# A width-31 depthwise convolution as matmuls over 4 time phases x 32 channels, mixed with the projections around it

## The chip, the cores, the metric

One Trainium2 chip, all 8 cores, one sequence of the batch on each core; nothing is exchanged between cores. The metric is the device time in microseconds (us) of the slowest core. Some runs here show a slow state, in which the cores of one die (or both) have a lower granted TensorE clock and take longer (the kernel before once took 7153.55 us, with clocks of 0.81 on die 0 and 0.90 on die 1, against 0.97 in its runs of 6121 to 6132 us).

## The reference, cut to what matters

Four layers on x of shape (8, 4096, 1024). Each has a token mixer and a feed-forward. The mixer of layer 1 is the Conformer block, which the change rewrites; layers 0 and 3 have a width-3 gated convolution, layer 2 pooling.

```python
def conformer_conv(h, w_pw1, b_pw1, conv_w, conv_b, ln_g, ln_b, w_pw2, b_pw2):
    p = h @ w_pw1 + b_pw1                            # (B, S, 2D)   first projection
    a, gt = jnp.split(p, 2, axis=-1)
    u = a * jax.nn.sigmoid(gt)
    v = causal_dwconv(u, conv_w) + conv_b            # each channel alone, 31 taps
    v = jax.nn.silu(layernorm(v, ln_g, ln_b))        # norm over the 1024 channels
    return v @ w_pw2 + b_pw2                         # second projection
# per layer: x += g1 * mixer(modulated rmsnorm(x));  x += g2 * swiglu(modulated rmsnorm(x))
```

## The kernel before

Channels lie on partitions, time on the free axis. A stage goes over the sequence in four passes of 1024 tokens; a pass is a list of *units* (one weight block each), each emitted in two halves of 512 tokens (`nt`). bf16 matmuls, fp32 residual. The kernel is traced by line, and all projections share one helper (line 601 before, 627 after), so groups are told apart by their tiles.

The Conformer block before, cut:

```python
def units_B(st):
    # first projection, 256 columns of weights per unit (line 705: sigmoid, line 707: product)
    ... e.activation(sg_t[:, k, :], gt, AF.Sigmoid, bias=..., scale=1.0)
    ... e.scalar_tensor_tensor(U[:, 30:542], a, bias, sg_t[:, k, :], ALU.add, ALU.mult)

    def mk_conv(j):                      # channel chunk j: 31 diagonal weights of 128x128 (line 720)
        def conv(pe):
            for kk in range(31):
                ins = pe.matmul(bk, slab[:, kk * 128:(kk + 1) * 128], U[:, kk:kk + 512],
                                start=(kk == 0), stop=(kk == 30))
    def emit_ln(nt, u):                  # fp32 mean, line 738: 8 matmuls of 512 columns with ones
        ...                              # then Square, two Vector passes, Silu (line 761)
    for m in range(4):
        mk_in(m); mk_conv(2 * m); mk_conv(2 * m + 1)
    unit(st, emit_ln)
    for m in range(2):
        mk_out(m)                        # second projection + residual (lines 621, 623)
```

Work for the following pass (its loads of x, its RMS sums, its norm) and the conversions of later weights are *tasks* that are spread over the units and run after the second half of a unit:

```python
a, b = sts[k]["first"], sts[k]["end"]            # in units
spread(steps[:2], t0, t0 + 1)                    # the loads
spread(steps[2:12], t1, t2)                      # Square + sum (lines 511, 514)
spread(steps[12:], t2, b - LAG - ...)            # the norm
...
u["emit"](1, u["cell"])
for fn in todo.pop(j, []):                       # tasks once per unit
    fn()
```

The sum of the RMS norm is one matmul with a matrix of ones behind each Square: TensorE waits there when the Square comes late (121 us in layer 0, in the waits below).

Of the kernel before, what the change touches and what calls it, by code (L numbers as in the profile page):

```python
# [12 lines left out]
D = 1024  # L13
# [3 lines left out]
F = 2816  # L17
# [5 lines left out]
NEH = 96  # L23

def _vec_layout():
    off = {}
    n = 0

    def add(name, w=8):
        nonlocal n  # L30
        off[name] = n
        n += w

    for i in range(4):
        add(f"nmg{i}")
        add(f"nfg{i}")
        add(f"adab{i}", 48)
    for j in range(2):
        add(f"acw{j}", 24)
    add("bb1", 16)  # L40
    add("bcw", 248)
    add("bcb")
    add("blg")
    add("blb")
    add("bb2")
    add("psc")
    add("fg")
    add("invcnt", 64)
    return off, n
# [3 lines left out]
def _sub_slabs(i, part):  # L53
# [5 lines left out]
    if kind == 1:  # L59
        return [("bpw1", 4096), ("bconv", 3968), ("bconv", 3968)] * 4 + [("bpw2", 4096)] * 2  # L60
    return [("cgrp", 2048)]

def _slab_table():
# [3 lines left out]
    for i in range(4):  # L67
        for part in "MF":
# [64 lines left out]

def _pack_vecs(inp):
# [13 lines left out]
    put("bcw", np.concatenate([_colvec(inp["b_conv_w"][0][k]) for k in range(31)], axis=1))  # L148
    put("bcb", _colvec(inp["b_conv_b"][0]))
    put("blg", _colvec(inp["b_ln_g"][0]))  # L150
    put("blb", _colvec(inp["b_ln_b"][0]))
# [31 lines left out]
class Prog:  # L183
# [7 lines left out]
    def op(self, eng, fn, reads=(), writes=(), sem=None, inc=1, after=()):  # L191
# [33 lines left out]
        for b in writes:  # L225
# [4 lines left out]
STAGES = ([("M", 0, s) for s in range(NPAIR)] + [("F", 0, s) for s in range(NPAIR)]  # L230
          + [("M", 1, s) for s in range(NPAIR)] + [("F", 1, s) for s in range(NPAIR)]
          + [("CF", 2, s) for s in range(NPAIR)]
          + [("M", 3, s) for s in range(NPAIR)] + [("F", 3, s) for s in range(NPAIR)])

# [3 lines left out]
def build():  # L238
# [6 lines left out]
    ident_d = nc.dram_tensor("ident", [128, 128], F32, kind="ExternalInput").ap()  # L245
# [6 lines left out]
    with es:  # L252
# [7 lines left out]
        scr_t = sb("scr", [128, 5, 532], F32)  # L260
        tmp_t = sb("tmp", [128, 4, 512], F32)
        sg_t = sb("sg", [128, 2, 512], F32)
        ada_t = sb("ada", [128, 3, 512], F32)
        junk = sb("junk", [128, 512], BF16)
# [8 lines left out]
        haloB = sb("haloB", [128, 8, 30], BF16)  # L273
        haloC = sb("haloC", [128, 8, 15], F32)
        ones_bf = sb("ones_bf", [128, 128], BF16)
        ones_f = sb("ones_f", [128, 128], F32)
        ident_bf = sb("ident_bf", [128, 128], BF16)
        small = sb("small", [128, 20], F32)
        psum = es.enter_context(nc.psum_tensor("psum", [128, 8, 512], F32))
# [7 lines left out]
        semnames = ["pe", "act", "dve", "pool", "vec", "idn", "cin"]  # L287
# [23 lines left out]
        identb = Buf("ident")  # L311
        cbcb = Buf("cbc")
        junkb = Buf("junk")
        rawb = Buf("raw")
        modb = [[Buf(f"mod{i}_{q}") for q in range(6)] for i in range(4)]
        derb = [[Buf(f"der{i}_{q}") for q in range(3)] for i in range(4)]
        haloAb = [[Buf(f"hA{l}_{c}") for c in range(8)] for l in range(2)]
        haloBb = [Buf(f"hB{c}") for c in range(8)]
# [3 lines left out]
        ctr = dict(bank=0, tmp=0, sg=0, scr=0, ub=0)  # L322
# [6 lines left out]
        def bank():  # L329
            k = nxt("bank", 6)  # L330
            return psum[:, k, :], bankb[k]
# [8 lines left out]
        scr_flat = scr_t[:, :, :].rearrange("p a b -> p (a b)")  # L340

# [4 lines left out]
        def v32(t):  # L346
            return hid2[:, t * 1024:(t + 1) * 1024].bitcast(F32), [hidb[t][0], hidb[t][1]]

        def utile():
            k = nxt("ub", 6)  # L350
            return scr_flat[:, k * 272:(k + 1) * 272].bitcast(BF16), [scrb[q] for q in range(k * 272 // 532, (k * 272 + 271) // 532 + 1)]
# [10 lines left out]
        P.op("dve", lambda e: e.memset(ones_f[:, :], 1.0 / D), writes=[constb])  # L362
# [29 lines left out]
        for (part, i, s) in STAGES:  # L392
            for p in part.replace("C", "M"):
                for q in range(len(SLABS[(i, p)])):
                    seq.append((i, p, s, q))
        wstate = dict(loaded=0, used=0, done=0)

        def load_slab(g):
# [7 lines left out]
            elif s == 0 and name == "bconv":  # L406
                def mkdiag(e):
                    for kk in range(31):
                        ins = e.tensor_scalar(wring[:, k, kk * 128:(kk + 1) * 128], ident_bf[:, :], vcol("bcw", kk * 8 + bconv_chunk(q), 1), None, ALU.mult)
                    return ins  # L410

                P.op("dve", mkdiag, reads=[vecsb, identb], writes=[wb[k]])
# [6 lines left out]
        def bconv_chunk(q):  # L419
            n = 0  # L420
            for r in range(q):
                if SLABS[(1, "M")][r][0] == "bconv":
                    n += 1
            return n

# [5 lines left out]
        def next_slab(expect):  # L431
            g = wstate["used"]
            assert seq[g][0:2] == expect, (g, seq[g], expect)
# [10 lines left out]
        def ada_mul(i, t, src, bufs):  # L444
            eh = SECTIONS[t // 16] * 16 + t % 16
            hf = eh % 2
            P.op("dve", lambda e: e.scalar_tensor_tensor(junk[:, :], src, 1.0, cbc[:, hf * 512:(hf + 1) * 512], ALU.mult, ALU.mult,  # L447
                                                         accum_out=raw[:, eh:eh + 1]),
                 reads=bufs + [cbcb], writes=[junkb, rawb])
# [181 lines left out]
        def unit(st, fn, nslabs=0):  # L631
            units.append(dict(emit=fn, nslabs=nslabs, st=st, cell={}))

        def get_slab(u, nt, expect):
            if nt == 0:
                u["slab"] = next_slab(expect)
            return u["slab"]

        def units_A(st):
# [5 lines left out]
            def mk_in(j):  # L645
                def emit(nt, u):
                    slab, slabb = get_slab(u, nt, (i, "M"))
# [21 lines left out]
                unit(st, emit, 1)  # L669

            def mk_out(m):
                def emit(nt, u):
                    slab, slabb = get_slab(u, nt, (i, "M"))
# [4 lines left out]
                unit(st, emit, 1)  # L678
# [6 lines left out]
        def units_B(st):  # L685
            i, s, hk = st["i"], st["s"], st["hk"]
            g1 = modT[:, i, 16:24]
            h_rhs = lambda k, nt: hbuf[:, hk, k, tsl(nt)]
            ut = {}

            def mk_in(m):
                def emit(nt, u):
                    slab, slabb = get_slab(u, nt, (i, "M"))
                    for q in range(2):
                        j = 2 * m + q
                        U, Ub = utile()
                        ut[(j, nt)] = (U, Ub)
                        if s == 0 and nt == 0:
                            P.op("dve", lambda e: e.memset(U[:, 0:30], 0.0), writes=Ub)
                        else:  # L700
                            P.op("dve", lambda e: e.tensor_copy(U[:, 0:30], haloB[:, j, :]), reads=[haloBb[j]], writes=Ub)
                        a, ab = proj_group(slab, slabb, q * 256, 8, 512, h_rhs, hb[hk], nt)
                        gt, gtb = proj_group(slab, slabb, q * 256 + 128, 8, 512, h_rhs, hb[hk], nt)
                        k = nxt("sg", 2)
                        P.op("act", lambda e: e.activation(sg_t[:, k, :], gt, AF.Sigmoid, bias=vcol("bb1", 8 + j, 1), scale=1.0),  # L705
                             reads=[gtb, vecsb], writes=[sgb[k]])
                        P.op("dve", lambda e: e.scalar_tensor_tensor(U[:, 30:542], a, vcol("bb1", j, 1), sg_t[:, k, :], ALU.add, ALU.mult),  # L707
                             reads=[ab, sgb[k], vecsb], writes=Ub)
                        P.op("dve", lambda e: e.tensor_copy(haloB[:, j, :], U[:, 512:542]), reads=Ub, writes=[haloBb[j]])
                unit(st, emit, 1)  # L710

            def mk_conv(j):
                def emit(nt, u):
                    slab, slabb = get_slab(u, nt, (i, "M"))
# [299 lines left out]
```

## Time and profile before

| | kernel before |
|---|---|
| median of 3 runs (range) | 6277.73 us (6123.72 to 7171.87) |
| fastest run | 6123.72 us |
| layer 0: mixer, feed-forward | 648, 928 us |
| layer 1: Conformer block, feed-forward | 1019, 992 us |
| layer 2: pooling and feed-forward | 1576 us |
| layer 3 to the end | 957 us |

The stretches are means over the eight cores of the profiled run. Each feed-forward or pooling layer is counted from its first gate x up product, so a stretch holds the handover to the next one. Layer 1's Conformer block is a sixth of the time; the views that show why are in the prediction below. Two Vector operations, by groups (line, engine, operation, tiles, shapes, count; then busy us and mean ns of one; then the idle time before them and what ended it):

```profile
L707 DVE SCALAR_TENSOR_TENSOR scr<-psum,vecs_sb,sg 128x512 bf16<-128x512 f32 x64 | 48.1, 751 | 511.0 <-ACT sg L705 510.5
L623 DVE TENSOR_TENSOR xres<-xres,tmp 128x512 f32<-128x512 f32 x64 | 43.9, 692 | 64.3 <-ACT tmp L621 63.9 <-issue 0.3
```

And TensorE's largest wait in layer 0 (waits of core 5, 0 to 666 us; the sum in us, how many, and the longest):

```profile
PE psum L514 <- ACT sqr L511: 121.2, 32, 48.5
```

The Square of x comes late for the RMS sum 32 times, by 121 us in all, 48 of them in one wait at the start.

### The profile page before, as it was taken

The numbers are of one execution on the slowest core, as the hardware profiler recorded it, in microseconds if no ns is written. First come the engines' busy times: TensorE is split into PE (matmuls) and PEld (weight loads), VectorE is DVE, ScalarE is ACT, GpSimd is POOL, SyncE is SP. The second block draws the span as 40 slices with busy tenths as digits, with TensorE's granted clock in tenths as the row PEclk, the third lists the DMA queues.
The fourth block names the chain that finished last, engine by engine and source line by source line (L and its number), as shares of the span: only waits on it lengthen the run. The fifth ranks groups of instructions, "written<-read, shape, count | busy, mean of one in ns | idle before, by whom it ended". The sixth has DMA issues, their size and how long they took to land.

```text
span 6137.7 us, 75215 instructions; the slowest of 8 cores (6107.0 to 6137.7 us)
## 1 busy us (share of the span) xinstructions
PE 5627.6 (92%) x25408; PEld 2504.6 (41%) x25408; DVE 2323.0 (38%) x4470; ACT 1668.4 (27%) x2530; POOL 457.7 (7%) x854
## 2 busy tenths in 40 slices
PE   3788999999989888899999979788799999999998
PEld 1333444444434333344444434333344444444443
DVE  4565432332331312223323345453624665233232
ACT  2222222222142433422222232313231222223221
POOL 1111010110000000001101001010100010000000
PEclk9899999999999999999999989899999999999999
DMA  7887444543424333156555234343545453233232
GB/s 179 198 205 189 155 147 144 181 139 107 143 77 141 104 107 120 63 156 205 154 166 177 87 117 135 128 129 126 147 126 157 141 162 136 97 134 103 96 110 73
DMA packets 201833, 837.86 MB, mean 137 GB/s; under 512 B 24032, under 2 KB 24032, under 8 KB 170592
## 3 DMA queue, kind: packets, MB, share of 16 engines
q1 hardware_dynamic: 135744, 544.60, 27.1%
q0 software_dynamic: 65712, 288.45, 18.3%
q8 instruction: 211, 3.46, 0.2%
q14 instruction: 166, 1.36, 0.1%
HBM read 791.83 MB, written 218.37 MB: 165 GB/s over the span
## 4 chain that ended last, share of the span: by engine, by line
PE 82%; DVE 6%; DMA 4%; ACT 4%; issue 3%; SPq 1%; DVEq 0%; POOL 0%; ACTq 0%; POOLq 0%
PE psum L601 72%; PE psum L720 7%; PE psum L514 2%; DVE scr L564 1%; DMA ada<-adaw 1%; DMA xres<-xT 1%; ACT sqr L511 1%; DVE xres L616 1%; DVE tmp L530 1%; ACT hbuf L537 1%; PE psum L738 1%; DMA wring<-wpack 1%; DVE tmp L759 1%; DMA wring<-wbf 1%; ACT scr L551 1%
## 5 line engine op out<-in xcount | busy, mean ns | idle before, releaser
L601 PE MATMUL psum<-hbuf,wring 128*128 128x512 bf16 x15872 | 3505.5, 382 | 126.7 <-ACT hbuf L761 81.1
L601 PEld LDWEIGHTS psum<-hbuf,wring 128*128 128x128 bf16 x15872 | 1559.1, 98 | 2026.5 <-issue 192.0
L601 PE MATMUL psum<-hid,wring 128*128 128x512 bf16 x6656 | 1459.2, 379 | 11.9 <-DVE xres L616 11.7
L821 DVE TENSOR_TENSOR hid<-psum,sg 128x512 bf16<-128x512 f32 x704 | 485.9, 692 | 1798.7 <-PE psum L601 1608.5
L601 PEld LDWEIGHTS psum<-hid,wring 128*128 128x128 bf16 x6656 | 651.6, 98 | 799.3 <-issue 17.0
L820 ACT ACTIVATE sg<-psum 128x512 f32<-128x512 f32 x704 | 419.0, 597 | 1676.3 <-PE psum L601 1618.2
L616 DVE SCALAR_TENSOR_TENSOR xres<-psum,modT,xres 128x512 f32<-128x512 f32 x384 | 279.2, 748 | 655.6 <-PE psum L601 655.6
L514 PE MATMUL psum<-sqr,ones_bf 128*128 128x512 bf16 x576 | 208.6, 400 | 321.3 <-ACT sqr L511 312.2
L511 ACT ACTIVATE sqr<-xres 128x512 bf16<-128x512 f32 x576 | 338.0, 623 | 519.6 <-DVE xres L616 322.7
L720 PE MATMUL psum<-scr,wring 128*128 128x512 bf16 x1984 | 444.6, 384 | 37.4 <-DVE scr L707 37.2
L537 ACT ACTIVATE hbuf<-tmp,modT 128x512 bf16<-128x512 f32 x448 | 303.5, 721 | 644.9 <-DVE tmp L530 636.2
L530 DVE SCALAR_TENSOR_TENSOR tmp<-xres,der,rstd 128x512 f32<-128x512 f32 x512 | 354.9, 745 | 15.5 <-ACT rstd L521 15.4
L592 POOL DMA_DIRECT2D xd<-xres x384 | 209.1, 545 | 1854.8 <-DVE xres L616 1093.1
L442 POOL DMA_DIRECT2D ada<-adaw x362 | 195.7, 541 | 1630.4 <-DVE junk L447 1350.1
L720 PEld LDWEIGHTS psum<-scr,wring 128*128 128x128 bf16 x1984 | 192.9, 98 | 283.9 <-issue 59.0
L447 DVE SCALAR_TENSOR_TENSOR junk<-ada,cbc 128x512 bf16<-128x512 f32 x362 | 248.8, 687 | 97.0 <-DMA ada<-adaw 80.7
L514 PEld LDWEIGHTS psum<-sqr,ones_bf 128*128 128x128 bf16 x576 | 56.6, 98 | 457.7 <-issue 420.6
L707 DVE SCALAR_TENSOR_TENSOR scr<-psum,vecs_sb,sg 128x512 bf16<-128x512 f32 x64 | 48.1, 751 | 511.0 <-ACT sg L705 510.5
L657 ACT ACTIVATE sg<-psum 128x512 f32<-128x512 f32 x128 | 76.3, 596 | 568.3 <-PE psum L601 538.7
L658 DVE TENSOR_TENSOR scr<-psum,sg 128x512 f32<-128x512 f32 x128 | 88.6, 692 | 236.9 <-ACT sg L657 233.7
L725 ACT ACTIVATE hid<-psum,vecs_sb 128x512 f32<-128x512 f32 x64 | 43.9, 686 | 368.6 <-PE psum L720 362.3
L387 POOL DMA_DIRECT2D wbf<-wpack x93 | 47.3, 508 | 1179.1 <-PE psum L514 678.3
(66 smaller groups left out, 1600.7 us busy)
## 6 DMA issues: line engine op xcount, KB each, us to landing
wring<-wbf SPq DMA_DIRECT2D x214, 1024.0 KB, 5.4
xd<-xres POOLq DMA_DIRECT2D x384, 256.0 KB, 3.6
xres<-xd SPq DMA_DIRECT2D x96, 1024.0 KB, 13.8
ada<-adaw POOLq DMA_DIRECT2D x362, 256.0 KB, 4.8
wring<-wbf SPq DMA_DIRECT2D x128, 704.0 KB, 4.3
wbf<-wpack POOLq DMA_DIRECT2D x52, 1024.0 KB, 10.5
wring<-wbf SPq DMA_DIRECT2D x56, 768.0 KB, 6.4
wring<-wbf SPq DMA_DIRECT2D x24, 992.0 KB, 4.9
```

Of the source, the lines that this page charges most:

```text
L442: P.op(q, lambda e: e.dma_start(out=dst, in_=adaw[i, eh]), writes=bufs, sem=sem, inc=16)
L447: P.op("dve", lambda e: e.scalar_tensor_tensor(junk[:, :], src, 1.0, cbc[:, hf * 512:(hf + 1) * 512], ALU.mult, ALU.mult, accum_out=raw[:, ...
L511: P.op("act", lambda e: e.activation(sqr2[:, nt, k, :], xres[:, xk, c, tsl(nt)], AF.Square), reads=[xb[xk][c][nt]], writes=[sq2b[nt][k]])
L514: P.op("pe", lambda e: e.matmul(bk, ones_bf[:, :], sqr2[:, nt, k, :], start=(c == 0), stop=(c == 7)), reads=[sq2b[nt][k], constb], writes= ...
L530: P.op("dve", lambda e: e.scalar_tensor_tensor(tmp_t[:, tk, :], xres[:, xk, c, tsl(nt)], gs[:, c:c + 1], rstd_t[:, nt, :], ALU.mult, ALU.m ...
L537: P.op("act", lambda e: e.activation(hbuf[:, hk, c, tsl(nt)], tmp_t[:, tk, :], AF.Identity, bias=sh[:, c:c + 1], scale=1.0), reads=[tmpb[t ...
L592: P.op("pool", lambda e: e.dma_start(out=xd[s, nt, c], in_=xres[:, xk, c, tsl(nt)]), reads=[xb[xk][c][nt]], writes=[xdb[s][nt][c]], sem=f" ...
L601: ins = pe.matmul(bk, slab[:, k * stride + col0:k * stride + col0 + 128], rhs_fn(k, nt), start=(k == 0), stop=(k == kchunks - 1))
L616: P.op("dve", lambda e: e.scalar_tensor_tensor(xs, bk, gvec, xs, ALU.mult, ALU.add), reads=[bkb] + deps, writes=[xb[xk][c][nt]])
L720: ins = pe.matmul(bk, slab[:, kk * 128:(kk + 1) * 128], U[:, kk:kk + 512], start=(kk == 0), stop=(kk == 30))
L820: P.op("act", lambda e: e.activation(sg_t[:, k, :], gt, AF.Silu), reads=[gtb], writes=[sgb[k]])
L821: P.op("dve", lambda e: e.tensor_tensor(hid(f, nt), up, sg_t[:, k, :], ALU.mult), reads=[upb, sgb[k]], writes=[hidb[f][nt]])
```

## The change

Its intent: the 31 diagonal weights waste 127 of 128 entries. Regrouping 128 channels x 512 tokens into 4 groups of (32 channels x 4 time phases) makes a 128x128 weight dense over pairs of phases; 31 taps become 9 shifts of 4 tokens. The regrouping is a shuffle from SBUF to SBUF by DMA (4 transfers per 128 channels), on the way in (`uP`) and back (`hbuf`). The products in front of the shuffle and the residual after it write or read in phase order, with fp32 steps of 16 bytes. The layer norm of pass s then runs under the first projection of pass s+1, and the second projection of pass s is mixed into the convolution of pass s+1. The sigmoid becomes a tanh, the mean is first added up on GpSimd. Tasks are placed by half units everywhere. The conversions of the projection and feed-forward weights of layer 1 move to the feed-forward of layer 0.

Cut to its core:

```diff
-                    for kk in range(31):
-                        ins = e.tensor_scalar(wring[:, k, kk*128:(kk+1)*128], ident_bf[:, :], vcol("bcw", ...), None, ALU.mult)
+                    for gg in range(2):                                    # line 440: 2 of 128x1152
+                        ins = e.tensor_tensor(wring[...], cmask[...], wtab[:, 2*q+gg, :, :]..., ALU.mult)
...
+                    for nt in range(2):                                    # units_B1: first projection
+                        gt, gtb = proj_group(...); a, ab = proj_group(...)
+                        P.op("act", ... sg_t <- AF.Tanh(gt, scale=0.5))                        # line 753
+                        P.op("dve", ... tmp_t <- a + bias)                                     # line 756
+                        P.op("dve", ... U3[:, :, nt*128:(nt+1)*128] <- (sg (t q)->q t + 1) * tmp (t q)->q t)   # line 758
+                    def shuffle(e):                                        # line 764
+                        return [e.dma_start(out=uP[:, 4*j+gg, 8:264], in_=U[gg:128:4, :]) for gg in range(4)]
+                    P.op("sp", shuffle, ...)
...
+                        for d in range(NSH):                               # units_B2, line 790; NSH = 9
+                            ins = pe.matmul(bk[:, 0:256], slab[:, par*CW+d*128:par*CW+(d+1)*128], uP[:, g, 8-d:264-d], ...)
+                    P.op("dve", ... vgroup(g) <- bk[:, 0:256] + bias)      # line 797
+                    P.op("act", ... AF.Square)                             # line 801
+                    P.op("pe", ... two 256-column sums of squares)         # lines 805, 806
+                    P.op("pool", ... acc += vpair(m))                      # line 813
...
+            def app(m):                                                    # ln_tasks, 16 per pass
+                P.op("dve", ... T3 <- V3 - Mt);  P.op("dve", ... T3 <- T3 * Rt)     # lines 846, 848
+                for h in range(2):
+                    P.op("act", ... AF.Silu)                               # line 852
+                if m % 2 == 1:
+                    P.op("sp", shuffle, ...)                               # line 859, hbuf <- hid
...
+                run(seq2[:6] + b3[:1] + seq2[6:11] + b3[1:] + seq2[11:])   # convolution + second projection
...
+            spread(tasks[1:], 2 * n0 + 1, 2 * n0 + 6)                      # norm, in half units of the first projection
...
+                for fn in todo.pop(2 * (idx - LAG), []):                   # tasks after each half unit
+                    fn()
                 u["emit"](1, u["cell"])
-                for fn in todo.pop(j, []):
+                for fn in todo.pop(2 * j + 1, []):
```

## The prediction

> **What bounds the kernel now.** I read the page's overview first, then the chain that ended last, then each stage by windows, and inside the stage that the change rewrites the groups, the waits and the timeline of TensorE. Layer 1 (the Conformer block: projection, width-31 convolution, layer norm, output projection) lies between the first convolution matmul at 1601 us and shortly after the last layer-norm matmul at 2581 us. In the page's 40 slices (153 us each) that is slices 11 to 17:
>
> ```profile
> PE   3788999999989888899999979788799999999998
> DVE  4565432332331312223323345453624665233232
> DMA  7887444543424333156555234343545453233232
> ...
> PE psum L601 72%; PE psum L720 7%; PE psum L514 2%; DVE scr L564 1%; DMA ada<-adaw 1%; DMA xres<-xT 1%; ACT sqr L511 1%; DVE xres L616 1%; DVE tmp L530 1%; ACT hbuf L537 1%; PE psum L738 1%; DMA wring<-wpack 1%; DVE tmp L759 1%; DMA wring<-wbf 1%; ACT scr L551 1%
> ```
>
> TensorE is the bound: 82% of the chain is its matmuls. Vector and DMA have room in layer 1 (1 to 3 tenths and 1 to 4 tenths there), less in layer 0 at the start and in the pooling layer (slices 23 to 29), which the change hardly touches. The windows give the size of it: a feed-forward stage, all of layer 1, two of its four passes, and one layer-norm stretch.
>
> ```profile
> core 5: us, PE busy (x) PEld busy (x) DVE busy (x) ACT busy (x) POOL busy (x), PEclk, DMA share, GB/s
> 700.00:1550.00 850.00, 849.55 (x3931) 384.36 (x3930) 255.74 (x481) 202.10 (x314) 81.94 (x152) 1.00 0.45 146
> 1600.00:2600.00 1000.00, 858.15 (x3684) 373.65 (x3683) 269.71 (x633) 356.42 (x505) 38.42 (x72) 0.95 0.35 105
> 1850.00:2100.00 250.00, 216.08 (x932) 94.34 (x931) 61.27 (x114) 89.69 (x128) 10.66 (x20) 0.95 0.40 114
> 2100.00:2350.00 250.00, 213.90 (x918) 93.06 (x917) 59.88 (x112) 90.71 (x129) 9.59 (x18) 0.95 0.34 102
> 1775.00:1850.00 75.00, 53.93 (x199) 22.70 (x198) 37.94 (x58) 48.15 (x67) 7.03 (x13) 0.86 0.30 91
> ```
>
> Feed-forward: TensorE never idle, 850/3931 = 0.2162 us per 512-column matmul. Layer 1: one pass of 1024 tokens takes 250 us, TensorE idles some 35 of them and the granted clock falls to 0.95, to 0.86 around the layer norm, where idle is. The groups and the waits say what fills and what interrupts it:
>
> ```profile
> L720 PE MATMUL psum<-scr,wring 128*128 128x512 bf16 x1984 | 444.6, 384 | 37.4 <-DVE scr L707 37.2 <-ACT scr L751 0.2
> L738 PE MATMUL psum<-hid,ones_f 128*128 128x512 f32 x128 | 62.7, 592 | 0.0
> L720 PEld LDWEIGHTS psum<-scr,wring 128*128 128x128 bf16 x1984 | 192.9, 98 | 283.9 <-issue 59.0
> ...
> PE psum L601 <- ACT hbuf L761: 81.1, 8, 10.3
> PE psum L720 <- DVE scr L707: 37.2, 20, 2.4
> PE psum L514 <- ACT sqr L511: 18.2, 16, 1.4
> ```
>
> The convolution (L720) is 1984 matmuls, 31 taps with 127 of 128 entries of each diagonal weight zero. The fp32 mean of the layer norm (L738) is 64 matmuls, recorded as 128, 62.7/64 = 0.98 us each. L761 is the layer norm's Silu: eight times, twice a pass, TensorE waits 10 us for it before the output projection, because nothing else is ready.
>
> [...] the new shuffles move exactly 512-byte rows. The trace has no such packet to check. [...] the new phase-reordering Vector operations read fp32 with a 16-byte step. No operation of the kernel before does, so their cost is open.
>
> **The change part by part**, per pass of 1024 tokens.
> *Convolution.* Channels are regrouped as 4 time phases x 32 channels, so a 128x128 weight is dense over 4x4 phases and 9 shifts replace 31 taps: 32 groups x 9 = 288 matmuls of 256 columns,[...] against 16 x 31 = 496 x 0.2162 = 107.2.
> *Layer-norm sums.* Squares: [...] (16 x 0.2162 = 3.5 before). The mean is first added up on GpSimd over 16 tiles, then 2 fp32 matmuls of 256 columns, about 1.0 us, against 16 x 0.98 = 15.7.
> *Unchanged.* First projection 256 x 0.2162 = 55.3, second 128 x 0.2162 = 27.7, RMS sums 16 x 0.2162 = 3.5.
> TensorE per pass: 122.4 us against 212.9; four passes 490 against 851 (858 busy in the window), so 361 us less work.
> *Idle.* The norm of pass s now runs under the first projection of s+1, and the second projection of s is mixed into the convolution of s+1 (of the last pass into the feed-forward). The 35 us of idle per pass, and the low clock behind it, should mostly go: up to another 170 us.
>
> What the other engines then have to do in 122 us. *Vector*, by its rows (a 128x8 operation 168 ns, 128x512 692: so 1.02 ns per element, 128x256 about 0.43 us): 16 x (0.69 + 0.75) in the first projection, 32 x 0.43 evictions, 32 x 0.69 norm, 16 x 0.69 residual, 16 x 0.745 next pass's norm = 82 us[...]. *ScalarE*: 16 x 0.69 tanh, 16 x 0.62 squares, 32 x 0.55 Silu, 16 x 0.775, 16 x (0.62 + 0.72), tables some 6 = 84 us. *GpSimd*: 15 adds, 16 stores: not a bound. *DMA*: convolution weights 16 x 0.59 = 9.4 MB (they are nine 128-wide blocks per group of 32 channels now, and each is used for only 1 us), projections 4.2 + 2.1, two loads of x 8.4, two shuffles 2.1 each, the store 4.2. From the page:
>
> ```profile
> q1 hardware_dynamic: 135744, 544.60, 27.1%
> q0 software_dynamic: 65712, 288.45, 18.3%
> ```
>
> q1 takes 0.271 x 6137.7/544.6 = 3.05 us per MB over the 16 engines, q0 3.89. So 28.3 x 3.05 + 4.2 x 3.89 = 103 us[...]. This is the tightest neighbour, and bursty: in the first projection (55 us) fall its weights, both x loads and both shuffles, 16.8 MB or about 60 us, all in one in-order queue ahead of the first convolution weights; the ring of four slabs covers only three units of 2.1 us there.
>
> *Sum for layer 1.* Pass 0 has no second projection to mix in, and Vector builds the weights: 32 operations of 128x1152, each 168 + 1.02 x 1144 = 1.34 us, most inside its convolution. There Vector has 24 x 1.34 + 14 + 12 = 58 us against 38 of TensorE, so pass 0 is 55 + 58 + 5 for the handover = 118. Passes 1 to 3: 122.4 each if TensorE were the only bound; with DMA at 116, bursts, and Vector evictions that share a queue with the norm, I choose 15% more, 141 each, 423. The last second projection costs 28 in the feed-forward. Together 569, against 1020 before (1600 to 2600 and about 10 at either end): 451 less.
>
> The rest: conversions of the layer-1 feed-forward weights move into the layer-0 feed-forward, where DMA is at 0.45 and TensorE full; tasks are placed in half units; pooling keeps its idle. I count zero. The fast run of before is 6124 us (the profiled one 6138; the other two of the three, 6278 and 7172, I take for the slow state). 6124 - 451 = 5673; I say 5665 as half-unit placement may give a little.
>
> **Rivals.**
> (a) Weight loads do not hide behind 256 columns. [...] If they ran in series, 1152 + 128 matmuls each cost 0.1 us more: +125 us, 5790.
> (b) DMA becomes the bound. For: 116 of 122 us, weights used once per load, eight cores at it. Against: windows of the kernel before reached 261 GB/s, and 32.5 MB in 141 us is 230. At 165 us a pass: +72 us, about 5740.
> (c) Vector becomes the bound of the first projection: [...] the norm's 22 squeezed into five of eight half units. +10 a pass, 5700.
> (d) Everything hides, a pass takes 124 us: 5610.
> (e) Only the matmul work goes and the waits come back elsewhere: 361 saved, 5765.
> None leads near 6000; for "same" the passes would have to stay above 225 us.
>
> **Range and chances.** Centre 5665; (d) with pass 0 at its TensorE time gives the low end, 5570; (a) gives the high end, 5790. Faster by over 2% 0.97, within 2% 0.02, slower 0.01 (layer 1 is a sixth of the span and loses 42% of its matmul time).
>
> **What would show it.** The convolution group should have 1152 matmuls at 0.11 to 0.12 us of busy time each; 0.2 says (a). A pass should repeat every 125 to 155 us with granted clock near 1.00, the wait for the Silu gone. TensorE waits for convolution weights with a DMA share of 0.9 or more say (b); waits for PSUM evictions in the first projection, and the two reordering operations well above 0.75 us, say (c). Pass 0's convolution should last about 60 us with Vector nearly full. I am wrong if layers 0, 2, 3 or the feed-forwards change by more than some 30 us.

What no trace of the kernel before shows is cut from the prediction, at the marks; its sums were made with it. The sum of matmul work, 122.4 us a pass, has 31.4 us for the convolution and 3.5 for the squares in it, from a time per 256-column matmul for which the trace had no row. Half of the 0.2162 us measured for 512 columns gives 31.1 and 3.5, as an estimate; the changed kernel then showed 0.109 us a matmul. The 38 us of pass 0, the 1 us for which a weight is used and the units of 2.1 us come from the same time. Two allowances were not shown: 13 us of DMA for the 512-byte rows (103 us without it, 116 with it; the "about 60 us" is an estimate between 51, at 3.05 us per MB for 16.8 MB, and 64 with it) and 18 us of Vector for the 16-byte steps (82 us without it, 100 with it), which gave rival (c) 54 us of Vector's work in the first projection. The totals: 118 + 423 + 28 = 569 us for layer 1, 451 less, and 5665 us. The 15% in them and the 0.55 us for a Silu of 128x256 (0.593 us in the changed kernel) were estimates.

## The result, and the profile after

Four runs of the changed kernel took 5699.14 us in the median (5695.94 to 5700.44). The kernel before, run four times beside it, took 6200.73 us (6123.05 to 7171.87) with slow runs among them. The ratio of the fast runs is 0.9306 (95% interval 0.9284 to 0.9329). Ratios here are the mean time of one kernel's fast runs over that of the other's of the same rounds, so not quite the ratio of the medians quoted.

The time is 34 us above the predicted 5665 and inside its range. The stretches tell less well of it:

| stretch, mean of cores, us | before | after | predicted | measured |
|---|---|---|---|---|
| layer 0, mixer | 648 | 614 | 0 | -34 |
| layer 0, feed-forward | 928 | 928 | 0 | 0 |
| layer 1, Conformer block | 1019 | 625 | -479 | -394 |
| layer 1, feed-forward (with the last second projection) | 992 | 1019 | +28 | +27 |
| layer 2, pooling and feed-forward | 1576 | 1540 | 0 | -36 |
| layer 3 to the end | 957 | 960 | 0 | +3 |
| sum | 6120 | 5686 | -451 | -434 |

Two errors nearly cancel: layer 1 gave 84 us less than I said, and layers 0 and 2, for which I counted zero, gave 70 (the 8 us between the sum, 5673, and the predicted 5665 were all that I allowed for them). The rest of this document is about those two.

The page of the profiled execution (5694.1 us), first its slices (busy tenths in 40 equal stretches, now 142 us each), then the chain that ended last:

```profile
PE   3889999999988888999999797979899999999998
DVE  4667432332285655333224454545326663223222
DMA  7888576854345655666442344435445543233132
...
PE psum L627 78%; PE psum L540 2%; DMA xres<-xT 2%; DVE tmp L556 1%; PE psum L790 1%; DMA wring<-wbf 1%; DVE aux L590 1%; DMA wring<-wpack 1%; ACT sqr L537 1%; DMA aux<-adaw 1%; ACT hbuf L563 1%; DVE xres L642 1%; DVE tmp L848 0%; DVE tmp L846 0%; ACT L546 0%
```

Layer 1 is now slices 12 to 16: TensorE 8 tenths there, Vector 5 to 8 where it had 1 to 3, DMA 4 to 6. The convolution (line 790) fell from 7% of the chain to 1%, the projections rose from 72% to 78%. Windows of core 5 (columns as in the prediction: length; busy us and counts of PE, PEld, DVE, ACT, POOL; granted clock, DMA share, GB/s): pass 0's convolution, and passes 1 to 3 together:

```profile
1592.00:1682.00 90.00, 63.70 (x396) 40.44 (x394) 80.82 (x85) 35.92 (x56) 34.72 (x15) 0.85 0.36 133
...
1682.00:2165.00 483.00, 395.28 (x2148) 217.08 (x2146) 293.62 (x391) 231.51 (x367) 91.03 (x93) 0.91 0.62 206
```

Over whole windows nothing is full except Vector in pass 0 (80.8 of 90 us). In passes 1 to 3 TensorE is busy 82% of the time at clock 0.91, Vector 61%, DMA 0.62: no engine is the bound all along, TensorE is interrupted. But these are averages: in the first projection of pass 1 the DMA engines are full for 30 us (and as long in passes 2 and 3, at shares of 1.03 and 1.01). Three windows of 10 us, same columns:

```profile
1700.00:1710.00 10.00, 8.34 (x40) 3.63 (x38) 8.26 (x12) 5.52 (x10) 0.00 (x0) 1.00 1.01 314
1710.00:1720.00 10.00, 7.93 (x35) 3.34 (x34) 8.08 (x12) 4.42 (x8) 0.00 (x0) 0.94 1.00 324
1720.00:1730.00 10.00, 9.60 (x40) 3.98 (x39) 8.19 (x12) 4.42 (x8) 0.00 (x0) 0.89 1.06 325
```

The groups show what the new operations cost:

```profile
L790 PE MATMUL psum<-aux,wring 128*128 128x256 bf16 x1152 | 160.3, 292 | 37.5 <-DMA wring<-wbf 17.4 <-DVE wring L440 8.4 <-ACT sg L753 7.1
L881 DVE TENSOR_TENSOR xres<-xres,tmp 128x512 f32<-128x512 f32 x64 | 69.4, 1100 | 67.8 <-ACT tmp L878 67.7
L758 DVE SCALAR_TENSOR_TENSOR hid<-sg,tmp 128x512 bf16<-128x512 f32 x64 | 69.2, 1082 | 31.8 <-ACT sg L753 26.0 <-DVE tmp L756 1.4
L440 DVE TENSOR_TENSOR wring<-cmask,wtab 128x1152 bf16<-128x1152 bf16 x32 | 51.8, 1658 | 0.0
```

The two operations with 16-byte steps take 1082 and 1100 ns against 751 and 692 for their counterparts of before (the one of 751 had an operand in PSUM, so the step is not all that differs there); the weight builder takes 1.66 us on average. That average hides two kinds. First the shortest, median and longest of its 32 operations (ns), then the same where an experiment below moves them into layer 0's feed-forward; then two pairs of them in the timeline of Vector, and the GpSimd addition (the sum for the mean) that runs beside the second pair:

```profile
L440 DVE TENSOR_TENSOR wring<-cmask,wtab x32: 1340/1350/2423, 1566.6 to 1665.0; 128x1152 bf16<-128x1152 bf16 x32
L1131 DVE TENSOR_TENSOR aux<-cmask,wtab x32: 1346/1352/1358, 881.6 to 1435.3; 128x1152 bf16<-128x1152 bf16 x32
...
1603.52 2.61 DVE L440 TENSOR_TENSOR wring<-cmask,wtab 128x1152 bf16<-128x1152 bf16 x2
1617.28 3.69 DVE L440 TENSOR_TENSOR wring<-cmask,wtab 128x1152 bf16<-128x1152 bf16 x2
1617.51 2.24 POOL L813 TENSOR_TENSOR hid<-hid 128x512 f32<-128x512 f32 x1 [4.59 <-DVE hid L797]
```

The 11 weight operations with no GpSimd addition beside them took 1.34 to 1.36 us. Of the 21 that overlap one, nine took 2.42 and one 1.63. It goes both ways: the additions take 1.26 to 1.29 us with neither these operations nor the norm of the next pass (line 556) beside them, up to 4.18 otherwise, and 23 of the 64 norm operations in layer 1, all beside an addition, took 1.75 to 1.77 us where the others took 0.73 to 0.81. So many of the sums on GpSimd and of these Vector operations take longer where they overlap. No run takes the sums away, so what this costs in passes 1 to 3 stays open.

The convolution's group mean (292 ns) is the mean length of records that overlap (1152 of them make 336 us in 160.3 us of busy time); its busy time over its count is 160.3/1152 = 0.139 us, with stretches at half clock in it: behind a gap of 5.49 us nine matmuls took 2.08 us at a granted clock of 0.50 (from 1765.44 us), where nine took 1.15 us at 1.00 (from 1773.63 us). What interrupts TensorE from 1543 to 2174 us (waits of core 5):

```profile
PE psum L540 <- ACT sqr L537: 31.6, 10, 8.0
PE psum L790 <- DMA wring<-wbf: 17.4, 7, 5.5
PE psum L805 <- ACT hid L801: 15.6, 10, 2.7
PE psum L627 <- ACT sg L753: 14.4, 9, 2.3
PE psum L627 <- DMA wring<-wbf: 12.2, 3, 10.4
```

The one large wait (81 us for the layer norm's Silu) has become many small ones: for the Square of the next pass's x, for convolution weights, for the squares of the convolution's own output, for the tanh, and (in the groups above) for weights that Vector builds. Two of them in the timeline (start, length, engine, line, operation, shapes, count, idle before and what ended it), and the convolution where nothing interrupts it:

```profile
1717.77 8.75 PE L627 MATMUL psum<-hbuf,wring 128*128 128x512 bf16 x32 [2.07 <-ACT sg L753]
1745.18 1.10 PE L540 MATMUL psum<-sqr,ones_bf 128*128 128x512 bf16 x2 [7.01 <-ACT sqr L537]
1754.66 2.13 PE L790 MATMUL psum<-aux,wring 128*128 128x256 bf16 x18
```

18 convolution matmuls, each with a new weight, run in 2.13 us: 0.118 us each, to the end of the last. The matmul behind them starts at 1756.63 us, 1.97 us after the first: 0.109 each. But 32 projection matmuls (6.9 us at the 0.2162 us of before) took 8.75 us and 2.07 more of waiting for a tanh.

The start and end times of all matmul records divide passes 1 to 3 of core 5 (1675.4 to 2157.7 us, 161 us a pass). From 1682 to 2154 us, 362 of 472 us are matmuls at their pace; with 7 more before 1682, that is 123 a pass, against 122.4 in the prediction. The rest is 74 us of gaps over 1 us, 9 of shorter ones, and 26 of matmuls at half clock (granted 0.50, as in the nine above), which follow gaps of over 1 us, though six of 1.42 to 2.06 us have none behind them: 36 us a pass, where I had put 19.

### The profile page after: what moved, and what is told of

It is laid out like the page before. It is cut to its first block, busy times and chain, and to the rows that moved or that the text cites. A ratio compares the mean times of both kernels' runs of the same rounds, so it can differ in the third digit from the quotient of the medians.

```text
span 5694.1 us, 73906 instructions; the slowest of 8 cores (5674.9 to 5694.1 us)
## 1 busy us (share of the span) xinstructions
PE 5264.6 (92%) x24528; PEld 2412.1 (42%) x24528; DVE 2461.0 (43%) x4314; ACT 1620.5 (28%) x2507; POOL 558.4 (10%) x916
## 3 DMA queue, kind: packets, MB, share of 16 engines
q14 instruction: 166, 1.36, 0.1%
## 4 chain that ended last, share of the span: by engine, by line
PE 81%; DVE 7%; DMA 5%; ACT 3%; issue 3%; SPq 0%; DVEq 0%; POOL 0%; ACTq 0%; POOLq 0%
PE psum L627 78%; PE psum L540 2%; DMA xres<-xT 2%; DVE tmp L556 1%; PE psum L790 1%; DMA wring<-wbf 1%; DVE aux L590 1%; DMA wring<-wpack 1%; ACT sqr L537 1%; DMA aux<-adaw 1%; ACT hbuf L563 1%; DVE xres L642 1%; DVE tmp L848 0%; DVE tmp L846 0%; ACT L546 0%
## 5 line engine op out<-in xcount | busy, mean ns | idle before, releaser
L556 DVE SCALAR_TENSOR_TENSOR tmp<-xres,der,rstd 128x512 f32<-128x512 f32 x512 | 388.9, 788 | 16.3 <-ACT rstd L547 16.3
L468 POOL DMA_DIRECT2D aux<-adaw x362 | 195.5, 541 | 1342.3 <-DVE aux L473 1120.2
L473 DVE SCALAR_TENSOR_TENSOR aux<-aux,cbc 128x512 f32<-128x512 f32 x362 | 247.3, 683 | 116.9 <-DMA aux<-adaw 115.0
L790 PE MATMUL psum<-aux,wring 128*128 128x256 bf16 x1152 | 160.3, 292 | 37.5 <-DMA wring<-wbf 17.4
L686 DVE TENSOR_TENSOR aux<-psum,sg 128x512 f32<-128x512 f32 x128 | 88.6, 692 | 193.1 <-ACT sg L685 184.5
L790 PEld LDWEIGHTS psum<-aux,wring 128*128 128x128 bf16 x1152 | 118.2, 104 | 70.9 <-issue 43.8
L813 POOL TENSOR_TENSOR hid<-hid 128x512 f32<-128x512 f32 x60 | 99.6, 1660 | 410.0 <-DVE hid L797 409.5
L577 ACT ACTIVATE aux<-tmp,modT 128x512 f32<-128x512 f32 x64 | 46.2, 722 | 301.7 <-DVE tmp L556 301.7
```

Source lines behind the costliest of these rows:

```text
L468: P.op(q, lambda e: e.dma_start(out=dst, in_=adaw[i, eh]), writes=bufs, sem=sem, inc=16)
L473: P.op("dve", lambda e: e.scalar_tensor_tensor(src, src, 1.0, cbc[:, hf * 512:(hf + 1) * 512], ALU.mult, ALU.mult, accum_out=raw[:, eh:eh ...
L556: P.op("dve", lambda e: e.scalar_tensor_tensor(tmp_t[:, tk, :], xres[:, xk, c, tsl(nt)], gs[:, c:c + 1], rstd_t[:, nt, :], ALU.mult, ALU.m ...
L790: ins = pe.matmul(bk[:, 0:256], slab[:, par * CW + d * 128:par * CW + (d + 1) * 128], uP[:, g, 8 - d:264 - d], start=(d == 0), stop=(d == ...
```

## The experiments

The kernel before ran (fast runs 6119.9 to 6131.5 us). Two theories stood at the start. For the gain outside layer 1: the placement of tasks in half units makes it (theory A), or something else in the change does, the moved conversions for instance. For the loss inside it: the in-order queues of Vector and ScalarE are filled at the wrong moments (norm, tanh, Square), or the DMA queue holds up the weights, or the mixing itself costs. That one operation holds up those behind it is seen in the changed kernel's trace (core 5): before the product of line 758 Vector stands 1.32 to 1.40 us for a tanh, four times from 1706 to 1737 us, with norm operations behind it, and ScalarE stands 4.11 to 4.14 us for the norm before a Silu, three times from 1718 to 1741 us, with a tanh or a Square behind it.

### Half units in the kernel before

```diff
-            a, b = sts[k]["first"], sts[k]["end"]
+            a, b = 2 * sts[k]["first"], 2 * sts[k]["end"] - 3          # all positions in half units
...
                 u["emit"](0, u["cell"])
+                for fn in todo.pop(2 * (idx - LAG), []):
+                    fn()
...
-                for fn in todo.pop(j, []):
+                for fn in todo.pop(2 * j + 1, []):
```

> The kernel before with nothing of the new convolution, only its background work (loads and norms of the next stage, modulation products, weight conversions) placed after every half unit as in the changed kernel instead of after every whole unit. The traces of before and after put layer 0's mixer at 666 and 616 us, and the pooling layer with its feed-forward at 1576 and 1540 us, though neither was meant to change. Theory A (the placement does it): 60 to 100 us under the 6124 of before, so 6025 to 6065, with layer 0's mixer ending near 620. Theory B (something else in the change does it: fewer conversions at that time, modulation written in place, other buffers): 6105 to 6140.

Only one run escaped the slow state: 6059.22 us. In all others but one, one die stayed undisturbed; undisturbed cores took 6039 to 6058 us against 6096 to 6130 for those of the kernel before. The undisturbed die of the profiled run in the view by cores (the other die took 6826 us at a clock of 0.845), and then the wait in layer 0 of core 4, which is on it, first in the kernel before (0 to 652 us), then here (0 to 616 us):

```profile
die 1 (median of its cores): 6050.7 us, clock 0.976
```

```profile
PE psum L514 <- ACT sqr L511: 112.1, 32, 45.3
```

```profile
PE psum L514 <- ACT sqr L511: 99.6, 24, 47.0
```

Layer 0's mixer took 607 to 616 us on die 1 (648 before), the pooling layer 1544 (1576 before), the rest within some 5 us what it took before. On the same core the wait for the Square fell from 112.1 to 99.6 us, in 24 waits instead of 32. Theory A holds: half-unit placement alone gives these gains, without any of the convolution. How it does is shown only in part: the 12.5 us of this wait are a third of the 36 us by which core 4's layer 0 is shorter.

### Whole units outside layer 1 in the changed kernel

```diff
-                todo.setdefault(lo + (t * n) // len(tasks), []).append(fn)
+                h = lo + (t * n) // len(tasks)
+                if not 2 * sts[("B1", 1, 0)]["first"] <= h < 2 * sts[("F", 1, 1)]["first"]:
+                    h |= 1                                 # as before: after the second half only
+                todo.setdefault(h, []).append(fn)
```

> The mirror: the changed kernel with the background work outside layer 1 put back after whole units. Theory A: 60 to 100 us over 5699, so 5760 to 5800. Theory B: 5685 to 5715.

5761.7 and 5764.61 us, some 65 above the changed kernel; layer 0's mixer 633 to 653, pooling 1570 to 1581, layer 1 unchanged at 620 to 626. The layer-0 wait of core 5 (0 to 651 us), first in the changed kernel (0 to 616 us), then here:

```profile
PE psum L540 <- ACT sqr L537: 96.2, 25, 47.4
```

```profile
PE psum L540 <- ACT sqr L537: 121.3, 33, 46.1
```

The same gain goes away when the half units do. Here the wait (25 us of the 35 on this core) makes most of it. The two runs agree from both sides: some 65 us of the change have nothing to do with the convolution.

### The norm spread over nine half units, not five

```diff
-            spread(tasks[1:], 2 * n0 + 1, 2 * n0 + 6)
+            spread(tasks[1:], 2 * n0 + 1, 2 * n0 + (9 if s < NPAIR - 1 else 6))
```

> The changed kernel with the layer norm of passes 0 to 2 spread over eight half units of the next first projection instead of five. Theory C (Vector and ScalarE, with the norm squeezed in among the PSUM evictions, set the pace of the first projection: half units of 9.15 us against 6.9 us of matmuls): each of three passes gains 8 to 15 us, so 5655 to 5675. Theory D (DMA, at 0.99 of its engines in that stretch, sets the pace): 5690 to 5705.

5690.03 and 5683.88 us; a third, 5735.74, had die 1 at a clock of 0.964 (the ratio, 0.9309, interval 0.9198 to 0.942, is of all three). On die 0 of this third, the profiled one, layer 1 took 610 to 615 us (625): some 13 less, where I had expected 24 to 45. The waits of core 0 in passes 1 to 3, first in the changed kernel (1670 to 2151 us), then here (1664 to 2126):

```profile
PE psum L540 <- ACT sqr L537: 26.0, 7, 8.0
PE psum L790 <- DMA wring<-wbf: 22.4, 9, 5.2
PE psum L627 <- ACT sg L753: 17.7, 9, 2.3
```

```profile
PE psum L540 <- ACT sqr L537: 42.5, 9, 7.4
PE psum L790 <- DMA wring<-wbf: 10.5, 7, 2.8
PE psum L627 <- ACT sg L753: 1.4, 3, 0.5
```

The wait for the tanh goes (17.7 to 1.4 us) and that for the convolution weights halves; in their place the wait for the Square grows from 26.0 to 42.5. The norm in the first projection does crowd the two in-order engines, but moving it later moves most of the wait with it.

### The norm's Silu one step later

```diff
-                for h in range(2): P.op("act", ... AF.Silu ...)            # right behind its two Vector passes
+                late.append(lambda: silu(m, tk, T))
+                while len(late) > (1 if m < 15 else 0):
+                    late.pop(0)()                                          # the Silu of the step before
```

> The changed kernel with each Silu of the norm issued one step later, so that the in-order ScalarE has not to wait for Vector's last norm operation before it can do the next tanh; the amount of work is the same. In the trace Vector waits 1.4 us for the tanh in each of these half units. Theory C1 (the waits between the two in-order queues make the excess): 15 to 35 us less, 5665 to 5685. Theory C2 (the sheer work of Vector does): 5690 to 5705. Theory D: the same as C2.

All runs were disturbed somewhere (5889 to 6337 us; the one of 5921.47 had a clock of 0.932). Undisturbed dies took 5665 to 5682 us against 5672 to 5699 for the changed kernel's, about 13 less. Layer 1, during which no core was disturbed, took 607 to 612 us, 16 less; core 0's wait for the tanh fell from 17.7 to 5.9 us and that for convolution weights from 22.4 to 12.9, while the wait for the Square stayed (26.5). ScalarE reaches the tanh sooner when it does not first stand in front of a Silu whose input Vector has not finished (4.14 us, before the Silu at 1731.49 us, on core 5 of the changed kernel). The direction is as expected and the size at the lower edge; with no undisturbed run this rests on cores of one die, and on the combined kernel below.

### Convolution weights built in the feed-forward before

```diff
-            elif s == 0 and name == "bconv":
+            elif False:                                   # pass 0 now loads its weights, as passes 1 to 3 do
...
+        lo, hi = span("F", 0)
+        spread(prebuild(), lo + 40, hi - 20)              # 32 Vector operations and 16 stores, in layer 0's feed-forward
```

> The changed kernel with the convolution weights built by Vector during the feed-forward of layer 0 (through the idle scratch region, 32 operations of 1.66 us each) and stored to HBM, so that pass 0 loads them as the other passes do. Theory E (building them binds pass 0: Vector full in 1620 to 1670 us, convolution 88 us long): 25 to 45 us less, 5655 to 5675, pass 0's convolution near 45 us. Theory F (the eviction, the GpSimd sums and the norm bind it anyway): within 10 us of 5699.

5679.39 and 5675.66 us (a third, 5697.7, had die 1 at a clock of 0.969 to 0.973); layer 1 took 603 us, 22 less, a little under what I had expected (25 to 45). Pass 0's convolution of core 5, which lasted 79 us:

```profile
1595.00:1647.00 52.00, 45.94 (x361) 34.60 (x360) 31.10 (x46) 29.09 (x47) 18.66 (x13) 1.00 0.65 211
```

52 us, at clock 1.00, with Vector at 31 us where the changed kernel has 74 from 1592 to 1671. Vector's 32 weight operations did bound pass 0, and layer 0's feed-forward hid them at no cost in time (it is as long with them as without). The gain is of two parts that this run does not separate: the work is gone from pass 0, and so are its collisions with the GpSimd additions (1.35 us an operation here, 1.66 there).

### No mixing: all of the second projection ahead of the convolution

```diff
-                run(seq2[:6] + b3[:1] + seq2[6:11] + b3[1:] + seq2[11:])
+                run(b3 + seq2)
```

> The changed kernel with the second projection of the pass before as one block ahead of the convolution instead of in two pieces within it; same work. Theory G (mixing is needed to feed the convolution: 0.59 MB of weights per 2.1 us is 277 GB/s[...]): three passes lose 8 to 20 us each, 5725 to 5760. Theory H (the ring and the DMA keep up, mixing is worth nothing): 5690 to 5710.

5705.3, 5702.79 and 5700.03 us: 5 us more, hardly a difference. Core 5, a stretch of convolution alone, and the wait that appears at the start of the second projection:

```profile
1793.00:1841.00 48.00, 44.82 (x359) 34.27 (x357) 32.67 (x47) 29.85 (x46) 22.20 (x19) 1.00 0.78 253
```

```profile
PE psum L627 <- DMA hbuf<-hid: 15.0, 1, 15.0
```

Convolution alone, fed with 0.59 MB for every 2.2 us (18 matmuls and 2 sums at 0.109 us), runs at its pace: 359 matmuls in 48 us, clock 1.00, DMA 0.78 at 253 GB/s. So the weights do not need the mixing, and rival (b) of the prediction is refuted for the convolution. For the first projection, into which the prediction put the burst, this run says nothing. What the mixing does is to give the norm and its shuffle time: without it, TensorE stands 15 us for the shuffled norm output, and gets most of it back afterwards.

### The shuffles issued from GpSimd's queue

```diff
-                    P.op("sp", shuffle, reads=Ub, ...)
+                    P.op("pool", shuffle, reads=Ub, ...)          # and likewise for hbuf <- hid
```

> The changed kernel with both shuffles issued from GpSimd's queue instead of the in-order queue that also issues the weight loads. Theory I (loads wait in the queue behind shuffles that wait for their data: TensorE waits 17.4 us for convolution weights and 12.2 us for projection weights in layer 1): 10 to 30 us less, 5670 to 5690. Theory D (the DMA engines themselves are the limit)[...]: 5695 to 5740.

5684.39 us (one fast run of six), layer 1 at 610, 15 less, the following feed-forward 4 less: within the expected range. Core 0's wait for convolution weights in passes 1 to 3 (1679 to 2139 us; 22.4 us in the changed kernel):

```profile
PE psum L790 <- DMA wring<-wbf: 6.0, 5, 1.5
```

In the changed kernel SyncE takes 2.45 us to issue the four parts of one shuffle (2.43 to 6.09 from 1680 to 1760 us), and before that its in-order queue waits for the product that the shuffle reads (line 758; 30 us from 1680 to 1850 us, 125 in layer 1), with loads of weights behind it. The end of such a wait, on core 5 of the changed kernel:

```profile
1757.01 2.45 SPq L764 DMA_DIRECT2D aux<-hid  x4
1759.61 0.47 SPq L450 DMA_DIRECT2D wring<-wbf  x1
...
1765.44 2.08 PE L790 MATMUL psum<-aux,wring 128*128 128x256 bf16 x9 [5.49 <-DMA wring<-wbf]
```

The load behind the shuffle is issued at 1759.61, when TensorE is about to run out of weights, and TensorE stands until 1765.44. That is order in the queue. But the run does not isolate it: issued from GpSimd, the same 16.8 MB of shuffles went out in 4096 packets of 4096 bytes instead of 32768 of 512, so their form changed too, in a stretch in which the DMA engines are full. How much of the gain is order and how much is the larger packets is not shown.

### Every convolution matmul twice

```diff
-                        for d in range(NSH):
+                        for d in list(range(NSH)) * 2:               # the second run overwrites the first: same result
```

> The changed kernel with each convolution group computed twice (1152 more matmuls, the second overwrites the first, result unchanged). Theory J (the convolution stretches of passes 1 to 3 are bound by TensorE, only pass 0 by Vector): 3 x 288 x 0.109 = 94 us more and pass 0 nearly free, 5780 to 5825. Theory K (the passes are bound by loads, evictions and norm all along): under 5750.

5743.98 and 5739.51 us: 43 us more for 1152 x 0.109 = 126 us of added matmuls. Core 5, a mixed stretch of the changed kernel, then the same here:

```profile
1732.00:1840.00 108.00, 84.45 (x496) 51.22 (x493) 59.71 (x79) 52.00 (x83) 28.71 (x30) 0.86 0.54 176
```

```profile
1736.00:1853.00 117.00, 107.15 (x781) 76.63 (x779) 60.30 (x79) 52.29 (x82) 28.70 (x30) 0.96 0.48 160
```

781 matmuls instead of 496 took 117 us instead of 108. Over the whole kernel two thirds of the added work fell into time in which TensorE had been waiting, or running at half clock. This stretch is the kindest one: on core 5 pass 0's convolution grew from 79 to 82 us, those of passes 1 to 3 by 10, 20 and 18 us of 31 added. So TensorE's own matmul time does not set the pace in pass 0, and only in part in passes 1 to 3; the rest is what TensorE waits for, of which the other experiments each show a part.

### The changed kernel again, and what the parts give together

The last call ran the changed kernel again, the three parts that had gained and cost nothing (Silu late, weights early, shuffles on GpSimd's queue), these with the wide norm, and these with the Squares of the next pass later as well:

```diff
-            spread(steps[2:12], lo - 3, mid)                     # only in the last of the four
-            spread(steps[12:], mid, hi + 1)
+            d = 5 if s < NPAIR - 1 else 3
+            spread(steps[2:12], lo - 3 + d, mid + 2)
+            spread(steps[12:], mid + 2, hi + 1)
```

> The changed kernel itself, unchanged, on the same chip as the three combinations, so that a few tens of us can be told apart: 5690 to 5705 in the fast state, layer 1 at 620 to 630 us on every undisturbed core.

5697.75 and 5696.7 us, ratio 0.9303 (0.928 to 0.9325): the result repeats.

> The changed kernel with three of the parts together: Silu one step later, convolution weights built ahead, both shuffles on GpSimd's queue. Alone they took 14, 22 and 16 us off layer 1 and off the feed-forward behind it. Theory L (independent waits): 40 to 55 us, 5645 to 5660. Theory M (they stand for the same slack, the next wait takes over): 20 to 30 us, 5670 to 5680.

5630.04, 5634.92 and 5630.62 us, ratio 0.9196 (0.9178 to 0.9214): 65 us under the changed kernel. In layer 1 with its feed-forward (means of cores) it is 65 us less, where the single gains are 18 (Silu late), 21 (weights early) and 19 (GpSimd's queue), 59 together. It is the best version found. The Conformer block takes 564 us (625). Core 0 in passes 1 to 3, the three waits that matter here (1590 to 2140 us; lines are one higher in this kernel):

```profile
PE psum L541 <- ACT sqr L538: 27.4, 7, 8.1
PE psum L806 <- ACT hid L802: 18.0, 12, 2.7
...
PE psum L628 <- ACT sg L754: 6.1, 9, 0.9
```

The mixed stretches last 91, 89 and 89 us (101, 99 and 97 on core 0 of the changed kernel), pass 0's convolution 50; over passes 1 to 3 the granted clock is 0.95. The wait for the Square is what is left, as large as it was.

> The combination with the norm over eight half units as well. The wide norm alone took 13 us off layer 1, but moved waits to the sums of squares (42 us of TensorE's waits against 26). Theory L: 5 to 12 us under the combination. Theory M (the late norm and the squares of the next pass now meet on ScalarE at the start of the convolution): within 5 us of it or slower.

5641.91 and 5637.09 us, ratio 0.9208 (0.9186 to 0.923): no better, 8 us worse on average; the wait for the Square is 35.3 us. Once the Silu is late, the wider norm has nothing left to gain.

> As the combination with the wide norm, with the squares of the next pass begun five half units later, after the norm has ended. If TensorE's 7 to 8 us waits for a Square at the end of each first projection come from the norm still in ScalarE's queue ahead of it, they go: 15 to 25 us under the combination with the wide norm, 5620 to 5640. If they come from the load of x, they stay: within 5 us.

5639.44, 5635.08 and 5652.18 us, ratio 0.9215 (0.9189 to 0.9241). The wait for the Square stayed, at 39.9 us. It was not tested cleanly: in the trace ScalarE still executes the norm's Silus until 1724.2 us, waiting for Vector between them, and the Square follows at 1724.6, with x long loaded. The load is not the cause; whether a Square free of those Silus would end the wait, the shift was too small to show.

## Why the prediction was right or wrong, point by point

**The matmul terms were right.** 122.4 us a pass was predicted and 123 measured. The convolution takes 0.109 us a matmul, its weight loads (104 ns on average) hidden: rival (a) is refuted. The wait of 81 us for the Silu went away, and the last second projection cost 27 us in the feed-forward, 28 predicted. For the other engines, Vector took 98 us a pass (82 predicted, 100 with the allowance), DMA 100 (103, and 116 with it), ScalarE 77; the 84 predicted for ScalarE was a slip, as its own terms add up to 78.

**The step that failed first: "I choose 15% more, 141 each".** A pass took 161 us. The excess over matmul work is 38 us and not 19; over three passes 482 us and not 423, 59 more. With that, the signs "125 to 155 us with granted clock near 1.00" failed too (161 us at 0.91). The allowance was for "DMA at 116, bursts, and Vector evictions that share a queue with the norm". As the bound of a whole pass, rival (b), DMA is refuted: share 0.62, about 100 us of 161 a pass, and convolution alone ran at pace at 253 GB/s. As a burst it is not: DMA is full for 30 us of each first projection, and TensorE's waits for weights in layer 1 (17.4 and 12.2 us on core 5) bound what that can directly cost. A 512-byte packet of the shuffles took 27 ns, a 2048-byte one 84 (medians), so 1.3 times as much per byte, though the small ones went from SBUF to SBUF and the larger ones not. The strided operations cost 1.44 and 1.59 times as much as their counterparts. Both are less than the allowances. What I had under-counted is nearest to rival (c), and I gave that +10 a pass: two in-order engines, each queue holding norm, tanh, eviction and Square in an order in which one waits for the other (Silu late: -13 us; the combined kernel), the shuffles in SyncE's queue (-19 us in layer 1 and its feed-forward, order and packet size not told apart), and the half clock that follows most of the gaps (26 us in three passes). The doubled convolution says the same from the other side, in part.

**The second: pass 0, "55 + 58 + 5 for the handover".** Its convolution took 79 us, not 58, with Vector busy in 73.9 of them. 28 of the 32 weight operations fell into it, where I had put 24: 45.4 us, not 32. At the 1.34 us that I had put for each they would be some 37; the size was right for the operation alone (1.35), and the other 8 us or so are its collisions with the GpSimd additions, which I had called "not a bound" and nothing more. Some 5 us are no error: the last 32 of the first projection's 256 matmuls run within this stretch, so that projection only looks 6 us shorter (49 us). Some 5 more are waits of Vector, in a stretch I had counted as Vector alone; its other work there was 3 shorter than I had put. Building the weights earlier brought 22 us back. At the start of the feed-forward, where I had put nothing, TensorE waited 10.4 us for a weight block. Passes +59, pass 0 +21, feed-forward +10, first projection -6: the 84, within a microsecond.

**The third: "The rest ... I count zero".** It was -34 in layer 0 and -36 in layer 2. I had read of half units in the diff and had dismissed them, without looking at what waits there; the 121 us of waits for the Square in layer 0 were to be seen in the trace. Both experiments on it agree: the placement alone does it, though the shorter waits for the Square are only a part of how (12.5 us of 36 on one core, 25 of 35 on another). By the prediction's own words it was wrong here ("if layers 0, 2, 3 or the feed-forwards change by more than some 30 us").

So the time came out near the centre partly by luck: 84 us missing in layer 1 and 70 not counted elsewhere nearly cancel. The mechanism was right, the direction was never in doubt, and the best kernel (5630 us) shows that even "everything hides" (5610) was not far out of reach.

**Open.** The wait of 7 to 8 us for the Square at the end of each first projection; the 10 us for the first weight block of the feed-forward; why the three parts together gain 6 us more than one by one; how much the GpSimd additions cost Vector in passes 1 to 3, and how much of the shuffles' gain is the queue and how much the packets. That the half clock follows from the gaps is read from their order in time, not tested by itself.

## What to carry to other kernels

When a change removes the bound of a stage, add up the matmul work for the floor, but take the allowance above it from the order of operations in each in-order queue (which one stands behind which, and whose input is not ready), not from shares of busy time: here nothing was above 62% on average apart from TensorE, the DMA engines were nevertheless full for 30 us of a pass, and a quarter of each pass was still lost. A line in the diff that only moves *when* tasks run deserves its own look at the waits of every stage it touches; it was worth some 65 us here, and can be had alone. Preparation that an engine does at the critical place (here weights built by Vector) should be put under a stage where that engine idles: that brought 22 us. And when a change gives work to an engine that is idle, look at whether the operations beside it get longer: beside the additions on GpSimd, nine Vector operations of otherwise 1.35 us took 2.42. When an experiment changes the queue of a transfer, look at its packets before you call the transfer the same: here 512 bytes became 4096.
